# A mixture-of-experts trunk on one core: PSUM handed over in two halves, and slot tables from one-hot products on chip

## The chip, the cores and the metric

The kernel runs on one core of a Trainium2 chip. The metric is the time of one execution in microseconds (us), as the device reports it. The engines are TensorE (PE, with its weight loads as PEld), VectorE (DVE), ScalarE (ACT), GpSimd (POOL) and SyncE (SP, which here only issues DMAs). Each runs its own instructions strictly in the order in which they were written, and waits on semaphores for the others.

## The reference

The layer takes x of 512 tokens by 1024 columns, mixes tokens by three head groups (a state space, pooling, block-sparse attention), adds the result to x, and then adds a mixture of experts. The second part, to which the change belongs, is this:

```python
t = rms_norm(x, norm2_g).reshape(-1, dm)
g_logits = t @ group_w + group_b              # 4 groups
g_sel = argmax(g_logits); g_wt = softmax(g_logits)[g_sel]
e_logits = (t @ router_w + router_b)[g_sel]   # 4 experts of that group
top_v, top_i = top_k(e_logits, 2); top_w = softmax(top_v)
comb[g_sel, top_i] = g_wt * top_w             # 512 x 16, two nonzero per token
act = silu(t @ w_gate[e]) * (t @ w_up[e]) * comb[:, e]
x = x + sum_e act @ w_down[e]
out = rms_norm(x, final_norm_g)
```

There are 16 experts with 256 hidden columns each. Their weights are 48 MB in float32 and are read once.

## The kernel before

**Slots and units.** Each expert has room for 96 token copies, so there are 1536 slots, handled as 12 units of 128. The 512 tokens are 4 tiles of 128, m = 0 to 3. Routing (`s_route`, line 1259) finds for each tile and each of a token's two choices i the slot number: `sv`, as float, and `slot_i`, as integer. A token's activations are kept as two float16 halves (`hl`, high and low), and every float32 product is made in three float16 passes.

**How tokens get to the slots.** Units 0 and 1 are gathered on chip: TensorE multiplies `hl` by one-hot matrices `sel`. Unit 0 (`s_gather`, line 1404) sums in four PSUM banks `gb` and is copied to `xts`; unit 1 (`s_gather_all`, line 1415) sums in four banks `gc` and is copied by ACT and DVE to `xp` (the rows show this buffer's earlier name). For units 2 to 11 GpSimd scatters the rows of `hl` into `x_scr` in DRAM (`scatter`, line 1250), and SP loads them back as `xr`; TensorE transposes them (`tx`).

**How a slot's token and weight are found.** The triple (row of the result, combining weight, token) of each token and choice is `mt_`. `s_meta_out` (line 1458) scatters the triples with eight indirect DMAs of GpSimd, 12 bytes a row, to `m_scr` in DRAM, which `s_clear` (line 804) has filled from an input with the values of an empty slot. `s_meta` (line 1643) loads the table back as `mt` and makes `tok` (the row to which a slot's result is scattered), `cw` (its weight), and `hot_e`, one-hot matrices for the last two units, from it.

**The expert stage.** For each unit u, `s_gate_up` (line 1584) multiplies the unit by gate and up weights into a PSUM bank `pg`; ACT and DVE make silu and product (`xs`); TensorE transposes it (`pta`); ACT and DVE split it into float16 halves (`aT`); TensorE multiplies by the down weights (`py`, two halves); ACT or DVE scales by `cw` into `ys`, and GpSimd scatters `ys` to `y_scr` in DRAM (`y_out`).

**The weights.** They come as 96 loads of 512 KB, six per expert, into five staging buffers `st_lde`. `st_lde_2_1` is the second half of the third matrix. ACT makes the high float16 half, DVE (a few times GpSimd) the low half, with one instruction each; only then is the staging buffer free for the load five places on. In this text gu5_0_1 is the split of expert 5's gate weights, second half.

**PSUM.** Up to the experts one pool `psA` holds all eight banks (`mm` x 3, `at` x 2, `tr` x 2, `po`; function `bank`). When routing is done and unit 1 is gathered, `s_memory` (line 1815) closes it and opens `psB` with `pg`, `pta`, `py`, `tx`.

**What sets the order.** A planner, class `Flow` (line 97), writes each engine's instructions. Every stage is a generator that yields an engine, the events that it needs and the tokens (buffers) that it takes; the planner always takes the one that its cost model would start first, with the rank that the stage was spawned with to break near ties. So an edit in one place can move instructions elsewhere. The real waits are semaphores, set from what each instruction reads and writes; and nearly all instructions of the trace carry the planner's line, L89.

Of the kernel before, what the change touches and what calls it, by code (L numbers as in the profile page):

```python
# [9 lines left out]
F16 = mybir.dt.float16  # L10
# [9 lines left out]
P = 128  # L20
D = 1024
# [40 lines left out]
C_W = C_COL + P  # L62
# [211 lines left out]
def hybrid_trunk_kernel(tc, a, out, cap=CAPACITY, dbg=None):  # L274
# [38 lines left out]
    m_scr = dram.tile([NSLOT + 2 * S, 3], F32, name="m_scr")  # L313
# [7 lines left out]
    phE, phP, phR, phQ, phA, phX = (ES() for _ in range(6))  # L321
# [29 lines left out]
    psA = phA.enter_context(tc.tile_pool(name="psA", bufs=1, space=PSUM))  # L351
    BANKS = {"mm": 3, "at": 2, "tr": 2, "po": 1}
    for k_, n_ in BANKS.items():
        fl.tokens(k_, n_)

    def bank(tag, name):
        return psA.tile([P, 512], F32, tag=tag, name=name, bufs=BANKS[tag])

# [435 lines left out]
    def s_clear():  # L794
# [9 lines left out]
        sp.dma_start(m_scr[0:NSLOT, :], a["meta0"])  # L804
# [442 lines left out]
    pads = cst.tile([P, 4 * NT + NE], F32, name="pads")  # L1247
# [11 lines left out]
    def s_route(m):  # L1259
        xg, h2T = (R_[m][k] for k in ("xg", "h2T"))  # L1260
        if m == 0:
            M["sm"] = M["R"].tile([P, NT, 170], F32, name="sm_r")
            M["sel"] = M["R"].tile([P, NT, NG, P], F16, name="sel")
# [12 lines left out]
        pool.tensor_scalar(rs16, rs, SA, None, ALU.mult)  # L1276
        fl.spawn(3, hl_out(m, xg, rs16))
# [5 lines left out]
        if m == NT - 1:  # L1283
# [7 lines left out]
        gm, kg, mg = R("gm", 1), R("kg", 4), R("mg", 4)  # L1291
# [8 lines left out]
        v.tensor_scalar(mg, kg, gk, -1.0, ALU.is_equal, ALU.add)  # L1300
        yield "dve"
        v.scalar_tensor_tensor(ms16.rearrange("p (g e) -> p g e", g=4),
                               mg.unsqueeze(2).to_broadcast([P, 4, 4]), -NEG,
# [28 lines left out]
        ok, sl, jk, sv = R("ok", 16), R("sl", 16), R("jk", 32), R("sv", 2)  # L1332
# [35 lines left out]
        yield "pool", (("hl", m),)  # L1368
# [26 lines left out]
    def gathered(g, banks, toks):  # L1395

        xT = xT_[g] = xts[0] if g == 0 else x2_t[NT - 1].bitcast(F16).rearrange("p (c n) -> p c n", n=P)
        for i, b in enumerate(banks):
            yield "dve" if i % 2 else "act"
# [15 lines left out]
    def s_gather_all(g):  # L1415

        toks = ("at", "at", "tr", "tr")
        yield "pe", (("gather", g - 1, NT - 1), "flag", ("acc", NT - 1)), toks
# [11 lines left out]
    def s_gates():  # L1430

        lg, gm, m8, ok, sl = (F_[n] for n in ("lg", "gm", "m8", "ok", "sl"))
        ge, gs, dn, co = (M["sm"][:, :, a_:b_] for a_, b_ in ((150, 155), (155, 156), (156, 157), (57, 89)))
# [15 lines left out]
        fl.spawn(0, s_meta_out())  # L1449
# [126 lines left out]
    def xt_out(u, h, tx, left):  # L1576
        yield "dve" if h else "act"
        (v.tensor_copy if h else act.copy)(xT_[u][:, h * KD:(h + 1) * KD, :], tx)
        fl.give("tx")
# [4 lines left out]
    def s_gate_up():  # L1584
        for u in range(NU):
            es = [e for e, _, _ in owners(u)]
            yield "pe", (("xT", u),) + tuple(("we", e, i) for e in es for i in range(2)), ("pg",)
            pg = B["ps"].tile([P, 512], F32, tag="pg", name=f"pg{u}", bufs=2)
# [14 lines left out]
    def s_down(u, pg):  # L1603
        ex_p, ps = B["ex"], B["ps"]
        es = [e for e, _, _ in owners(u)]
        ends = [e for e in es if last_unit[e] == u]
        yield "act", (), ("ex",)
# [8 lines left out]
        pt = ps.tile([P, 2 * P], F32, tag="pta", name=f"pta{u}")  # L1616
# [3 lines left out]
        yield "act"  # L1620
        aT = ex_p.tile([P, 2, 2, P], F16, tag="aT", name=f"aT{u}")
# [5 lines left out]
        ys = ex_p.tile([P, D], F32, tag="ys", name=f"ys{u}")  # L1627
        for nh in range(2):
            if nh and u < NU - 2:
                yield "pe"  # L1630
            py = ps.tile([P, 512], F32, tag="py", name=f"py{u}_{nh}", bufs=3)
# [8 lines left out]
        fl.give("ex")  # L1640
        fl.sig(*(("dend", e) for e in ends))

    def s_meta():
        yield "pool", ("meta", "B")
        mt = B["ex"].tile([P, NU, 3], F32, tag="mt", name="mt", bufs=1)
        pool.dma_start(mt, m_scr[0:NSLOT, :].rearrange("(u c) w -> c u w", c=P))
        fl.sig_dma("mt")
        yield "dve", ("mt",)
        B["tok"] = B["ex"].tile([P, NU], I32, tag="tok", name="tok", bufs=1)
        B["cw"] = B["ex"].tile([P, NU], F32, tag="cw", name="cw", bufs=1)  # L1650
        v.tensor_copy(B["tok"], mt[:, :, 0])
        v.tensor_scalar(B["cw"], mt[:, :, 1], ISC, None, ALU.mult)
        fl.sig("cw")
        for i in range(NL):
            for t in range(NT):
                yield "dve", (("dend", NE - 5),)
                if i == 0 and t == 0:
                    B["hot"] = page("p3", [P, NL, S], F16, "hot_e")
                v.tensor_scalar(B["hot"][:, i, t * P:(t + 1) * P], cpk[:, C_COL:C_COL + P],
                                mt[:, NU - NL + i, 2:3], -float(t * P), ALU.subtract, ALU.is_equal)  # L1660
# [103 lines left out]
    def y_out(u, nh, py, ys):  # L1764
# [19 lines left out]
        else:  # L1784
# [12 lines left out]
            fl.sig_dma(("y1", u))  # L1797


    phB, ph0 = ES(), ES()  # L1800

    def s_memory():
        yield "mem", ("dm", "epn", "sprev")
# [212 lines left out]
```

## Time and profile before

| | us |
|---|---|
| median of 3 runs | 458.46 |
| lowest, highest | 454.86, 460.24 |
| the profiled execution's own time | 455.13 |
| span of that execution | 453.3 |

| engine | busy us | share of the span |
|---|---|---|
| PE | 374.5 | 83% |
| DVE | 318.3 | 70% |
| PEld | 208.2 | 46% |
| ACT | 248.4 | 55% |
| POOL | 116.7 | 26% |

The mean granted clock of TensorE is 0.931 of full speed. 109.88 MB move by DMA, 242 GB/s over the span. The shares are means over parts of the kernel that have different limits; the part that the change touches lies between 255 and 320 us, so windows and timelines of that part say more than the totals. Start times in the rows count from the span's start. A pause stands in square brackets behind the row that ended it, with what released it; "remote" means that no other engine's or DMA's end was found for it.

### The profile page before, as it was taken

What the parts mean: (1) busy time and instruction counts of PE and PEld (TensorE: products, weight loads), DVE (VectorE), ACT (ScalarE), POOL (GpSimd) and SP (SyncE); (2) the same over time, 40 slices, a digit from 0 to 9 for tenths busy, and PEclk for the clock granted to TensorE, in tenths of its full rate; (3) what the DMA queues carried; (4) which work ended last, traced back from release to release, by engine and by line L of the source; (5) the groups of instructions that cost most, each with busy time, mean ns of one, the idle gap of its engine ahead of it and who ended that gap; (6) DMA issues with size and microseconds to landing.
All of it is one profiled execution on the core that took longest, in us unless ns stands there. A gap on an engine that the chain in (4) does not pass through costs nothing. (4 is left out here: it accounts for less than half of the span.)

```text
span 453.3 us, 8911 instructions
## 1 busy us (share of the span) xinstructions
PE 374.5 (83%) x3456; PEld 208.2 (46%) x3456; DVE 318.3 (70%) x638; ACT 248.4 (55%) x399; POOL 116.7 (26%) x202
## 2 busy tenths in 40 slices
PE   2899964399999999989999673699999795858992
PEld 1697531164446456444466463254545342413340
DVE  2789807955785877976689991548678778877383
ACT  4753203143658986875776530348677677575231
POOL 1248984402400100011117458003111001000010
PEclk9999995889999999999999668699999999969997
DMA  8912549998698598674395442558999999988933
GB/s 283 339 50 38 76 55 261 383 337 272 191 167 271 187 317 281 213 232 137 114 353 190 161 181 94 170 207 249 413 410 328 418 354 350 314 309 313 406 134 142
DMA packets 49153, 109.88 MB, mean 242 GB/s; under 512 B 4499, under 2 KB 25907, under 8 KB 49108
## 3 DMA queue, kind: packets, MB, share of 16 engines
q1 hardware_dynamic: 45652, 99.57, 66.8%
q0 software_dynamic: 2896, 9.47, 5.5%
q8 instruction: 28, 0.46, 0.4%
q10 hardware_dynamic: 560, 0.25, 0.3%
q14 instruction: 17, 0.14, 0.1%
HBM read 83.59 MB, written 25.70 MB: 241 GB/s over the span
## 5 line engine op out<-in xcount | busy, mean ns | idle before, releaser
L89 DVE SCALAR_TENSOR_TENSOR gu<-st_lde,gu 128x1024 f16<-128x1024 f32 x63 | 76.9, 1236 | 19.3 <-ACT gu L89 19.2
L89 PE MATMUL pg<-gu,xts 128*32 128x512 f16 (+1 forms) x912 | 64.9, 392 | 13.1 <-DVE xp L89 11.5
L89 ACT ACTIVATE gu<-st_lde 128x1024 f16<-128x1024 f32 x64 | 66.4, 1054 | 16.3 <-DMA st_lde<-in_moe_w_gate_dram 8.7
L89 PEld LDWEIGHTS <-xts 128*32 128x32 f16 (+1 forms) x912 | 28.0, 101 | 44.8 <-issue 22.0
L89 PE MATMUL px<-wo,cat 128*128 128x512 f16 x192 | 44.7, 379 | 0.0
L89 PE MATMUL py<-dn,aT 128*32 128x512 f16 (+1 forms) x480 | 37.9, 406 | 5.5 <-ACT aT L89 4.8
L89 DVE SCALAR_TENSOR_TENSOR dn<-st_lde,dn 128x1024 f16<-128x1024 f32 x30 | 37.5, 1256 | 5.9 <-ACT dn L89 5.9
L89 ACT ACTIVATE dn<-st_lde 128x1024 f16<-128x1024 f32 x32 | 33.2, 1054 | 7.2 <-DMA st_lde<-in_moe_w_down_dram 7.0
L89 PEld LDWEIGHTS <-hT 128*64 128x64 f16 (+1 forms) x384 | 31.2, 156 | 6.7 <-issue 2.9
L89 POOL DMA_INDIRECT y_scr<-ys,tok x10 | 10.4, 1040 | 87.7 <-ACT ys L89 84.4
L89 PE MATMUL ps_k<-hT,w_k 128*128 128x512 f16 x96 | 24.3, 406 | 10.0 <-ACT qk L89 10.0
L89 ACT ACTIVATE pr<-pr,nm 128x128 f32<-128x128 f32 (+3 forms) x32 | 17.9, 558 | 25.3 <-DVE nm L89 25.0
L89 PEld LDWEIGHTS <-cat 128*128 128x128 f16 x192 | 18.2, 99 | 21.3 <-issue 3.2
L89 PEld LDWEIGHTS <-aT 128*32 128x32 f16 (+1 forms) x480 | 14.1, 103 | 26.3 <-ACT aT L89 6.6
L89 PE MATMUL ps_v<-w_v,hT 128*128 128x256 f16 x192 | 24.7, 287 | 0.8 <-ACT hT L89 0.4
L89 PE MATMUL psS<-qk 64*64 64x128 f32 (+3 forms) x128 | 24.0, 474 | 0.0
L89 PE MATMUL ptp<-cpk,pr 128*128 128x128 f32 x80 | 14.9, 289 | 9.8 <-DVE rcp L89 7.0
L89 ACT COPY pts<-ptp 128x128 f32<-128x128 f32 (+3 forms) x32 | 13.4, 422 | 17.6 <-PE ptp L89 17.3
L89 PE MATMUL ps_q<-hT,w_q 128*128 128x512 f16 x96 | 22.6, 379 | 0.0
L89 POOL TENSOR_TENSOR dn<-st_lde,dn 128x1024 f16<-128x1024 f32 x2 | 4.9, 2463 | 65.8 <-ACT dn L89 65.8
L89 PEld LDWEIGHTS <-w_k 128*128 128x128 f16 x96 | 9.4, 102 | 22.4 <-issue 13.8
L89 PEld LDWEIGHTS ptp<-cpk,pr 128*128 128x128 f32 x80 | 9.2, 142 | 19.3 <-issue 15.5
(255 smaller groups left out, 715.1 us busy)
## 6 DMA issues: line engine op xcount, KB each, us to landing
st_lde<-in_moe_w_gate_dram SPq DMA_DIRECT2D x32, 512.0 KB
st_lde<-in_moe_w_up_dram SPq DMA_DIRECT2D x32, 512.0 KB
st_lde<-in_moe_w_down_dram SPq DMA_DIRECT2D x32, 512.0 KB
x_scr<-zero SPq DMA_DIRECT2D x12, 512.0 KB
xr<-x_scr SPq DMA_DIRECT2D x10, 512.0 KB
xp<-in_x_dram SPq DMA_DIRECT2D x8, 512.0 KB
y_scr<-zero SPq DMA_DIRECT2D x8, 512.0 KB
yr<-y_scr SPq DMA_DIRECT2D x4, 1024.0 KB
```

Of the source, the lines that this page charges most:

```text
L89: r = f(*args, **kw)
```

## The change

1. The PSUM pool is split. `psA` (banks `mm`, `po`) and `psC` (`at`, `tr`) take its place; at the hand-over `psB` (`pg` x 2, `pta`, `tx0`) opens once unit 0's copies are planned, and `psD` (`py` x 3, `tx1`) once routing, the new slot table and unit 1's copies are.
2. `m_scr`, its load, the eight scatters and the load back are gone. `s_places` makes on DVE, from the slot numbers `sv_`, one-hot rows: `place` (which of a unit's 128 slots) and `vals` (which unit, times the triple); eight float32 matmuls sum place x vals into a PSUM tile `pm`, 128 slots by 36 columns. `s_meta` reads `cw`, `tok` and the tokens for `hot_e` from `pm` by four DVE instructions. The constants `cpk` grow by 25 columns.
3. The scatters of tiles 1 and 2 on GpSimd wait until the last tile's 1/rms has been computed there.
4. The wait for the store of x2 to DRAM moves from unit 1's gather to its copies.

```diff
-    psA = phA.enter_context(tc.tile_pool(name="psA", bufs=1, space=PSUM))
+
     BANKS = {"mm": 3, "at": 2, "tr": 2, "po": 1}
+    HALF = {"mm": 0, "po": 0, "at": 1, "tr": 1, "pg": 0, "tx0": 0, "py": 1, "pta": 0, "tx1": 1}
+    psum = [es.enter_context(tc.tile_pool(name=n_, bufs=1, space=PSUM, side=s_))
+            for es, n_, s_ in ((phA, "psA", "left"), (phA2, "psC", "right"))]
...
-        sp.dma_start(m_scr[0:NSLOT, :], a["meta0"])
...
+        fl.sig(("rms", m))
...
-        yield "pool", (("hl", m),)
+        yield "pool", (("hl", m),) + ((("rms", NT - 1),) if m in (1, 2) else ())
...
-    def s_meta_out():
-        for m in range(NT):
-            yield "pool"
-            for i in range(2):
-                scatter(m, m_scr, mt_[:, m, i, :], i)
-        fl.sig_dma("meta")
+    def s_places():
+
+        K = 2 * NT
+        yield "dve", ("B0",), ("R", "R")
...
+        v.tensor_tensor(ge, sv.to_broadcast([P, K, NU + 1]), edge.unsqueeze(1).to_broadcast([P, K, NU + 1]), ALU.is_ge)
+        yield "dve"
+        v.tensor_reduce(cnt_u, ge, AX.X, ALU.add)
+        v.scalar_tensor_tensor(col, cnt_u, -float(P), sv, ALU.mult, ALU.add)
+        yield "dve"
+        v.tensor_tensor(oneh, ge[:, :, 0:NU], ge[:, :, 1:NU + 1], ALU.subtract)
+        yield "dve"
+        v.tensor_tensor(vals.rearrange("p k (w u) -> p k w u", w=3), oneh.unsqueeze(2).to_broadcast([P, K, 3, NU]),
+                        mt_.rearrange("p t i w -> p (t i) w").unsqueeze(3).to_broadcast([P, K, 3, NU]), ALU.mult)
+        for k in range(K):
+            yield "dve"
+            v.tensor_scalar(A[:, k], cpk[:, C_COL:C_COL + P], col[:, k], float(P), ALU.subtract, ALU.is_equal)
+        yield "pe", (), ("tx0",)
+        B["pm"] = psum[HALF["tx0"]].tile([P, 512], F32, tag="tx0", name="pm")
+        for k in range(K):
+            pe.matmul(B["pm"][:, 0:3 * NU], A[:, k], vals[:, k], start=(k == 0), stop=(k == K - 1))
+        fl.sig("placed")
...
     def s_meta():
-        yield "pool", ("meta", "B")
-        mt = B["ex"].tile([P, NU, 3], F32, tag="mt", name="mt", bufs=1)
-        pool.dma_start(mt, m_scr[0:NSLOT, :].rearrange("(u c) w -> c u w", c=P))
-        fl.sig_dma("mt")
-        yield "dve", ("mt",)
...
-        v.tensor_copy(B["tok"], mt[:, :, 0])
-        v.tensor_scalar(B["cw"], mt[:, :, 1], ISC, None, ALU.mult)
+        etok = B["ex"].tile([P, NL], F32, tag="etok", name="etok", bufs=1)
+        junk = B["ex"].tile([P, NU], F32, tag="junk", name="junk", bufs=1)
+        rows, gate, toks = (B["pm"][:, i * NU:(i + 1) * NU] for i in range(3))
+        v.tensor_scalar(B["cw"], gate, ISC, None, ALU.mult)
+
+        v.scalar_tensor_tensor(junk, rows, 0.0, cpk[:, C_JUNK:C_JUNK + NU], ALU.is_equal, ALU.mult)
+        v.scalar_tensor_tensor(B["tok"], rows, -1.0, junk, ALU.add, ALU.add)
+        v.tensor_copy(etok, toks[:, NU - NL:])
+        fl.give("tx0")
...
-        yield "mem", ("routed", ("xT", NG - 1))
+        yield "mem", (("xT", 0),)
+        fl.t = fl.ev["gather", 0, NT - 1]
+        phA.close()
+        psum[0] = phB0.enter_context(tc.tile_pool(name="psB", bufs=1, space=PSUM, side="left", reuse_waits="tile"))
+        for k_, n in (("pg", 2), ("pta", 1), ("tx0", 1), ("aT0", 1)):
+            fl.tokens(k_, n)
+        fl.sig("B0")
+        yield "mem", ("routed", "placed", ("xT", NG - 1))
         fl.t = fl.ev["gather", NG - 1, NT - 1]
```

The order of instructions moves in three places that matter here. On DVE, from the end of routing (`cov`) to the first product of unit 0 (`xs`), the kernel before has this; `gc` are unit 1's gather banks, `st_lde` the weight halves of expert 5:

```order
L89 TENSOR_TENSOR cov<-sm_r 128x4x16
L89 CAST tri_89<-cpk 128x128
L89 CAST xp_120<-gc_1_2977 128x512
L89 SCALAR_TENSOR_TENSOR gu_1_2759<-st_lde_0_1_2545,gu_0_2758 128x4x256
L89 CAST xp_120<-gc_3_2979 128x512
L89 SCALAR_TENSOR_TENSOR gu_1_2759<-st_lde_1_0_2560,gu_0_2758 128x4x256
L89 SCALAR_TENSOR_TENSOR gu_1_2759<-st_lde_1_1_2570,gu_0_2758 128x4x256
L89 SCALAR_TENSOR_TENSOR dn_3063<-st_lde_2_0_2641,dn_3063 128x1024
L89 SCALAR_TENSOR_TENSOR xs_121<-pg_3090,xs_121 128x256
```

And the changed kernel, from the small `vals` instructions to the next weight split:

```order
L91 CAST xp_122<-gc_1_2974 128x512
L91 TENSOR_TENSOR vals<-vals 128x96
L91 TENSOR_TENSOR vals<-vals,mt__137 128x288
L91 CAST xp_122<-gc_3_2976 128x512
L91 TENSOR_SCALAR place<-cpk,vals 128x128 x8
L91 SCALAR_TENSOR_TENSOR gu_1_2756<-st_lde_0_0_2539,gu_0_2755 128x4x256
L91 SCALAR_TENSOR_TENSOR xs_123<-pg_3061,xs_123 128x256
L91 TENSOR_SCALAR cw<-pm 128x12
L91 SCALAR_TENSOR_TENSOR junk<-pm,cpk 128x12
L91 SCALAR_TENSOR_TENSOR tok<-pm,junk 128x12
L91 COPY etok<-pm 128x2
L91 SCALAR_TENSOR_TENSOR gu_1_2756<-st_lde_0_1_2556,gu_0_2755 128x4x256
```

The weight splits stand one half later than before, the eight `place` and the four readings of `pm` stand among them, and `xs` of unit 0 stands ahead of four weight splits that it followed.

On PE, behind the last matmul of unit 0's `pg`, the changed kernel has the eight matmuls of `pm`, and then unit 1's `pg`:

```order
L91 MATMUL pg_3061<-gu_1_1791,xts_124 32x512
L91 MATMUL pm<-vals,place 128x36 x8
L91 LDWEIGHTS xp_122
L91 MATMUL pg_3190<-gu_0_1790,xp_122 64x512
L91 LDWEIGHTS xp_122
```

Before, unit 1's `pg` followed unit 0's directly. On POOL, the changed kernel has the last tile's 1/rms (four instructions, the first of which reads `ss`) ahead of the scatters of `x_scr` from tiles 1 and 2 (`slot_i`):

```order
L91 TENSOR_TENSOR xg_2732<-xp_122,g_1783 128x512
L91 TENSOR_TENSOR sm_r<-ss_85 128x1
L91 TENSOR_SCALAR sm_r<-sm_r 128x1
L91 TENSOR_TENSOR sm_r<-sm_r,nhalf 128x1
L91 TENSOR_SCALAR sm_r<-sm_r 128x1
L91 MEMSET pads 128x1
L91 DMA x_scr<-xp_121,slot_i 2560x2048
L91 MEMSET pads 128x1
L91 DMA x_scr<-xp_121,slot_i 2560x2048
```

Before, the first two of these scatters stood between `xg` and the four instructions.

## Rows read from the trace of the kernel before

**Rows 1.** The page's busy tenths of the whole span in 40 slices of 11.3 us each.

```profile
PE   2899964399999999989999673699999795858992
DVE  2789807955785877976689991548678778877383
DMA  8912549998698598674395442558999999988933
```

**Rows 2.** The view of windows: start:end, length, busy us of each engine (with the number of instructions), granted clock of TensorE, mean share of the DMA engines, GB/s.

```profile
270.00:280.00 10.00, 5.93 (x69) 5.85 (x70) 3.56 (x20) 0.69 (x2) 7.70 (x15) 0.79 0.30 109
280.00:290.00 10.00, 2.33 (x24) 1.03 (x27) 4.80 (x6) 4.24 (x5) 4.02 (x6) 0.56 0.19 20
...
320.00:390.00 70.00, 59.49 (x831) 28.71 (x824) 55.78 (x71) 49.98 (x62) 7.75 (x13) 0.98 1.00 378
```

**Rows 3.** The view of waits for 268 to 292 us: who waited for whom, total us, times, longest.

```profile
ACT xp L89 <- remote: 13.1, 1, 13.1
PE pg L89 <- DVE xp L89: 11.5, 1, 11.5
DVE xp L89 <- remote: 11.4, 1, 11.4
```

**Rows 4.** The timeline of PE: start, length, engine, line, operation, output <- inputs, count, and in brackets the pause before it and its releaser.

```profile
275.14 1.06 PE L89 MATMUL gc<-sel,hl 128*128 128x128 f16 x16
287.67 7.16 PE L89 MATMUL pg<-gu,xts 128*32 128x512 f16 x96 [11.48 <-DVE xp L89]
```

**Rows 5.** The timeline of ACT.

```profile
284.47 0.58 ACT L89 CAST xp<-gc 128x512 f16<-128x512 f32 x1 [13.12 <-remote]
```

**Rows 6.** The timeline of DVE, from routing's end to the first product of unit 0.

```profile
273.55 0.22 DVE L89 CAST tri<-cpk 128x128 f16<-128x128 f32 x1
285.19 0.69 DVE L89 CAST xp<-gc 128x512 f16<-128x512 f32 x1 [11.43 <-remote]
285.80 1.22 DVE L89 SCALAR_TENSOR_TENSOR gu<-st_lde,gu 128x1024 f16<-128x1024 f32 x1
...
289.80 1.22 DVE L89 SCALAR_TENSOR_TENSOR dn<-st_lde,dn 128x1024 f16<-128x1024 f32 x1
295.30 0.42 DVE L89 SCALAR_TENSOR_TENSOR xs<-pg,xs 128x256 f32<-128x256 f32 x1 [4.28 <-ACT xs L89]
```

**Rows 7.** The timeline of POOL: the first and the last of the eight `m_scr` scatters, and a weight split.

```profile
273.50 0.97 POOL L89 DMA_INDIRECT m_scr<-mt__134,slot_i  x1 [0.19 <-DVE sm_r L89]
...
282.35 0.96 POOL L89 DMA_INDIRECT m_scr<-mt__134,slot_i  x1 [0.19 <-issue]
...
309.86 2.80 POOL L89 TENSOR_TENSOR dn<-st_lde,dn 128x1024 f16<-128x1024 f32 x1 [22.63 <-ACT dn L89]
```

**Rows 8.** The DMA view of 276 to 284 us: all packets that moved in it.

```profile
DMA packets 223, 0.01 MB, mean 1 GB/s; under 512 B 223, under 2 KB 223, under 8 KB 223
```

**Rows 9.** The timeline of SP: the weight load 6_0_0, and the loads of the scattered rows of units 2 and 3.

```profile
287.08 0.35 SPq L89 DMA_DIRECT2D st_lde<-in_moe_w_gate_dram  x1
287.60 0.80 SPq L89 DMA_DIRECT2D xr<-x_scr  x2
```

**Rows 10.** Durations that serve as prices: PE's `pg` of unit 2 (two pieces) and `pl` of the first and the last tile, from its timeline; a DVE reading of 12 columns, from its timeline; and, from the view by tile, eight DVE one-hot instructions (ns: least, median, most; first and last start).

```profile
307.37 3.64 PE L89 MATMUL pg<-gu,xts 128*32 128x512 f16 x64
312.35 1.91 PE L89 MATMUL pg<-gu,xts 128*32 128x512 f16 x32
230.64 1.86 PE L89 MATMUL pl<-rw,h2T 128*128 128x20 f32 x16
257.17 3.58 PE L89 MATMUL pl<-rw,h2T 128*128 128x20 f32 x16
308.58 0.17 DVE L89 TENSOR_SCALAR cw<-mt 128x12 f32<-128x12 f32 x1
L89 DVE TENSOR_SCALAR hot_e<-cpk,mt x8: 274/283/325, 388.4 to 389.8; 128x128 f16<-128x128 f32 x8
```

**Rows 11.** The timeline of DVE, from unit 0's `aT` to the first split of expert 7, the rows with pauses and one copy.

```profile
299.42 0.42 DVE L89 SCALAR_TENSOR_TENSOR aT<-pta,aT 128x256 f16<-128x256 f32 x1 [1.43 <-ACT aT L89]
301.15 0.42 DVE L89 SCALAR_TENSOR_TENSOR xs<-pg,xs 128x256 f32<-128x256 f32 x1 [1.31 <-ACT xs L89]
304.69 1.23 DVE L89 SCALAR_TENSOR_TENSOR gu<-st_lde,gu 128x1024 f16<-128x1024 f32 x1 [3.12 <-ACT gu L89]
...
306.17 0.68 DVE L89 COPY xts<-tx 128x1024 f16<-128x1024 f16 x1
...
312.47 0.75 DVE L89 TENSOR_SCALAR ys<-py,cw 128x512 f32<-128x512 f32 x1 [1.80 <-PE py L89]
...
314.26 1.22 DVE L89 SCALAR_TENSOR_TENSOR gu<-st_lde,gu 128x1024 f16<-128x1024 f32 x1
```

**Rows 12.** The timeline of DVE: the last split of expert 15's down weights.

```profile
417.44 1.22 DVE L89 SCALAR_TENSOR_TENSOR dn<-st_lde,dn 128x1024 f16<-128x1024 f32 x1
```

**Rows 13.** The timelines of POOL and DVE around the last tile's 1/rms: a scatter, the first rms instruction, and DVE's logits of that tile.

```profile
257.25 2.65 POOL L89 DMA_INDIRECT x_scr<-xp,slot_i  x1
259.92 0.20 POOL L89 TENSOR_TENSOR sm_r<-ss 128x1 f32<-128x1 f32 x1
...
261.48 0.23 DVE L89 SCALAR_TENSOR_TENSOR sm_r<-pl,sm_r,rbias 128x20 f32<-128x20 f32 x1
```

More of the change, by code (lines that the diff above doesn't have):

```diff
@@ L61 @@
 C_COL = C_ELIM + NE
-C_W = C_COL + P
+C_EDGE = C_COL + P
+C_JUNK = C_EDGE + 13
+C_W = C_JUNK + 12
 def _free(ap):
@@ L319, in hybrid_trunk_kernel @@
     t_scr = dram.tile([8, HD * (VW + 1)], F32, name="t_scr")
-    phE, phP, phR, phQ, phA, phX = (ES() for _ in range(6))
+    phE, phP, phR, phQ, phA, phA2, phX = (ES() for _ in range(7))
     cst = pool_of(top, "cst")
@@ L356, in bank @@
     def bank(tag, name):
-        return psA.tile([P, 512], F32, tag=tag, name=name, bufs=BANKS[tag])
+        return psum[HALF[tag]].tile([P, 512], F32, tag=tag, name=name, bufs=BANKS[tag])
     gp_ = pool_of(phQ, "gp_", 1, "right")
@@ L1246, in hybrid_trunk_kernel @@
     F_ = {}
-    pads = cst.tile([P, 4 * NT + NE], F32, name="pads")
+    pads = cst.tile([P, 2 * NT + NU], F32, name="pads")
+    sv_ = cst.tile([P, NT, 2], F32, name="sv_")
     mt_ = cst.tile([P, NT, 2, 3], F32, name="mt_")
@@ L1456, in s_gates, with part @@
         fl.sig("routed")
-    def s_meta_out():
-        for m in range(NT):
-            yield "pool"
-            for i in range(2):
-                scatter(m, m_scr, mt_[:, m, i, :], i)
-        fl.sig_dma("meta")
+    def s_places():
+        K = 2 * NT
+        yield "dve", ("B0",), ("R", "R")
+        A, W = (M["R"].tile([P, D], F32, tag="xg", name=n, bufs=2) for n in ("place", "vals"))
+        A = A.rearrange("p (k c) -> p k c", k=K)
+        def part(c0, n):
+            return W[:, c0:c0 + K * n].rearrange("p (k n) -> p k n", k=K)
+        ge, cnt_u, col = part(0, NU + 1), part(K * (NU + 1), 1), part(K * (NU + 2), 1)
+        oneh, vals = part(K * (NU + 3), NU), part(K * (2 * NU + 3), 3 * NU)
+        sv = sv_.rearrange("p t i -> p (t i)").unsqueeze(2)
+        edge = cpk[:, C_EDGE:C_EDGE + NU + 1]
+        v.tensor_tensor(ge, sv.to_broadcast([P, K, NU + 1]), edge.unsqueeze(1).to_broadcast([P, K, NU + 1]), ALU.is_ge)
[15 more added lines that the diff above has]
+        fl.sig("placed")
     def hl_out(m, xg, rs16):
@@ L1615, in s_down @@
         yield "pe", (), ("pta",)
[L1616 removed]
+        pt = psum[HALF["pta"]].tile([P, 2 * P], F32, tag="pta", name=f"pta{u}")
         acv = ac.rearrange("p (c k) -> p k c", k=2)
@@ L1626, in s_down @@
         fl.sig(*(("dstart", e) for e in ends))
-        ys = ex_p.tile([P, D], F32, tag="ys", name=f"ys{u}")
+        ys = B["ex"].tile([P, D], F32, tag="ys", name=f"ys{u}")
         for nh in range(2):
@@ L1630, in s_down @@
                 yield "pe"
-            py = ps.tile([P, 512], F32, tag="py", name=f"py{u}_{nh}", bufs=3)
+            py = psum[HALF["py"]].tile([P, 512], F32, tag="py", name=f"py{u}_{nh}", bufs=3)
             i = 0
@@ L1817, in s_memory @@
         phQ.close()
-        phA.close()
+        phA2.close()
         B["ex"] = pool_of(phB, "ex", 2, "right")
         xts.extend(B["ex"].tile([P, 2 * KD, P], F16, name=f"xts{i}", bufs=1) for i in range(1, NXT))
-        B["ps"] = phB.enter_context(tc.tile_pool(name="psB", bufs=1, space=PSUM, reuse_waits="tile"))
-        for k_, n in (("pg", 2), ("pta", 1), ("py", 3), ("tx", 2), ("ex", 2), ("ys", 2)):
+        psum[1] = phB.enter_context(tc.tile_pool(name="psD", bufs=1, space=PSUM, side="right", reuse_waits="tile"))
+        for k_, n in (("py", 3), ("tx1", 1), ("aT1", 1), ("ys", 2)):
             fl.tokens(k_, n)
```

57 lines of the change are left out of this document (29 added, 28 removed).

## The prediction, made before the changed kernel was run

> **What bounds the kernel now.** I read the page's busy tenths first [rows 1], then ten-microsecond windows around the change [rows 2], then the list of waits of that stretch [rows 3], then the timelines of the engines there. The tenths show three regimes: TensorE nearly full until about 250 us, a dip after it, and from about 290 us a stretch in which the 16 DMA engines are full. The windows say how deep the dip is: in 270:280 and 280:290 the DMA share is 0.30 and 0.19, TensorE works 5.93 and 2.33 us of ten, and no engine is full in 280:290. In 320:390 the DMA share is 1.00: there the kernel takes the expert weights as fast as they come, so time lost in the dip is not won back later, nor is time won in the dip lost.
>
> In the waits one pause shows on three engines at once: PE 11.5, DVE 11.4, ACT 13.1 us [rows 3]. TensorE's row of gather matmuls for unit 1 (`gc`) ends at 276.20, and its next row, `pg` of unit 0, begins at 287.67 [rows 4]. What stands between them are the four copies of `gc` into `xp`. But ACT's first copy begins at 284.47 and DVE's at 285.19 [rows 5, 6], both "remote", 8 to 9 us after the matmuls' shown end, with nothing running on either engine. The one thing that fills these 8 us is GpSimd: eight `m_scr` scatters of about 0.96 us each from 273.50 on, the last at 282.35 [rows 7]; and the DMA view of 276:284 holds 223 packets with 0.01 MB, all from that queue [rows 8]. The sync engine's next weight load is issued only at 287.08 [rows 9], since the buffer it needs is freed by the DVE split at 285.80 [rows 6].
>
> **The change part by part, forecast.** I take it that the copies' start is tied to the `m_scr` scatters, and that it goes with them. For it: the scatters' packets fill just this pause, and an `x_scr` scatter such as that at 257.25, with far larger rows, runs beside a `pl` of TensorE whose result DVE reads 0.73 us after its end (260.75 to 261.48) [rows 10, 13].
>
> *PSUM halves.* `pg0` no longer needs the banks of `gc`, so it follows `gc` on TensorE at 276.2. Its price: `pg` of the unit behind took 3.64 + 1.91 = 5.55 us at full granted clock [rows 10], `pg0` itself 7.16 at a clock that was at the lower level (0.56 granted in 280:290, after the pause) [rows 2, 4]. With no pause ahead of it I take 5.55, 7.16 as the other end: `pg0` ends at 281.75 instead of 294.83, 13.1 earlier.
>
> *Places on VectorE.* After the shown end of `tri` at 273.77 [rows 6] it gets three small instructions (at most 0.3 each, as the 128x128 ones of rows 10) beside `gc`. From 276.2 on: copy 0.69, `oneh` 0.3, the 128x288 product (between 0.28 and the copy's 0.69; I take 0.69, the nearer in width), copy 0.69, eight `place` at 0.283 = 2.26 [rows 6, 10]: done at 280.8, under `pg0`. The split `gu5_0_0` ends at 282.0, `xs` from `pg0` at 282.6.
>
> *`pm`.* Eight fp32 matmuls with 36 columns. The nearest row is `pl`, eight fp32 matmuls (16 records) with 20 columns: 1.86 at the upper clock level, 3.58 at the lower [rows 10]. I take 1.86: 281.75 to 283.6. The four readings of `pm` stand on VectorE **ahead of the weight splits**; four times 0.17 (the `cw` row [rows 10]) gives 284.3, and the split behind them, `gu5_0_1`, ends at 285.5. It frees the buffer of the load of 6_0_0; before, that split ended at 287.02 [rows 6].
>
> *VectorE to the first split of expert 7.* From 285.5, in the new order: two `aT` and two `xs` at 0.42 (1.68), two `xts` at 0.68 (1.36), two `ys` at 0.75 (1.50), and eleven splits at 1.22 (13.42), of which one, `dn6_2_0`, ran on GpSimd before (2.80 us at 309.86 [rows 7]); 17.96 in all [rows 6, 11]. Back to back that ends at 303.5. Before, the stretch from 291.02 (end of the split at 289.80) to 314.26 held 11.94 us of pauses: 4.28 for `pg0`'s `xs`, which goes, and 1.43 + 1.31 + 3.12 + 1.80 = 7.66 for later matmuls and loads [rows 6, 11]. How much of the 7.66 stays no row shows: 0 to 7.66; I keep 4.5, rather over half, since `pg1`, `py` and the loads keep their lengths and only start sooner. The split of 7_0_0 then ends at 308.0 instead of 315.48 (314.26 + 1.22): **7.5 us earlier**, between 4.3 (all of 7.66 stays) and 12.0 (none stays).
>
> *Carrying it to the end.* From that split to the last, at 417.44 [rows 12], lie 53 others in 103.2 us, 1.95 each, in a stretch with DMA share 1.00: the whole of it shifts. TensorE follows the weights and closes the kernel behind them, at 9 tenths in the slices from 419 to 442 [rows 1]. I carry all 7.5.
>
> *The rest, at nothing.* The last tile's rms goes ahead of the scatters of tiles 1 and 2 on GpSimd. Its four rows begin at 259.92, right behind a scatter of 2.65 us, but DVE's `lg` at 261.48 also needs `pl`, on TensorE until 260.75 [rows 10, 13]: at most 0.7 is to be had. The scatters behind it slip by the 1.7 us of rms and whatever rms waits for; what they feed is loaded at 287.60 [rows 9], over 20 us later, and that cover hides them. Two more weight splits that GpSimd did go to VectorE long before the dip (2 x 1.22); VectorE is not full there in most tenths [rows 1], so 0, with +2.4 as the bound. The planner also reshuffles TensorE's attention part; with the same work, I bound it at 2 us either way, taken as 0. The first `y_scr` scatters come forward out of the full DMA stretch, which can only help a little: 0 to -1.
>
> **Sum.** 455.13 - 7.5 = 447.6 against the profiled execution. The median of the three runs, 458.46, stands 3.3 above that; measured from it the forecast is **451.0**.
>
> **The rivals.** *(b) The whole pause is won.* Nothing of the 7.66 stays and the PE wait of 11.5 is all gain: 458.46 - 11.5 = 447. For it: VectorE's pauses there are mostly waits for TensorE. Against: the eleven splits and the eight `place` do not shrink.
>
> *(c) The message stays late, TensorE is free.* The cause is not the scatters of `m_scr`; the copies still begin at 284.5 and 285.2, while `pg0` runs in the pause. Then DVE does copy, `oneh`, product, copy, `place` from 285.2 to 289.8, `pm` ends at 291.7, the readings at 292.4, `gu5_0_1` at 293.6; with the same 17.96 + 4.5 the split of 7_0_0 ends at 316.0, 0.6 later than before: **459**. What TensorE won is given back by VectorE. For it: "remote" names no cause, and a coincidence in time is all that ties the pause to the scatters.
>
> *(d) Slower: TensorE itself is late.* If `gc` really runs until 285, `pg0` is behind it at the lower clock level: 285.2 + 7.16 = 292.4, and `pm` comes after that, at the lower level 3.58: 296.0; the four readings and `gu5_0_1` end at 297.9, where before a split had freed that buffer at 287.02 without waiting for any matmul. With 17.96 + 4.5 the split of 7_0_0 ends at 320.4, 4.9 later: **463.4** (461.7 with `pm` at 1.86). It decides from the point where `pg0` ends later than about 288, since 7.5 is then used up. For it: the readings put a wait for TensorE ahead of the weight stream, which stood free of it. Against: the granted clock in 280:290 is 0.56, and TensorE's next work, `pg0`, was still at the lower level, as after a real pause [rows 2, 4]; matmuls that ran until 285 would rather have held it up.
>
> The row says 276.20 for the end of `gc` and 284.47 for the first copy. The Trainium skill, in "Perfetto Trace Analysis", section "Tensor Engine Instruction (MATMUL, LD_WEIGHTS)", says that a matmul's end in a profile is worked out from its size, and that the semaphore goes out only once PSUM has acknowledged the writes, which the profile doesn't show. By that rule the 276.20 need not be the end, and the sum would be rival (d)'s; by the row alone it would be the forecast's.
>
> **How the numbers follow.** Forecast 0.45, (b) 0.13, (c) 0.22, (d) 0.20. About 1% (4.6 us: under 453.9, over 463.0) is what a measurement of this kernel can tell. Faster by over 1%: nine tenths of the forecast and all of (b), 0.54, say 0.55. Slower by over 1%: about half of (d) and a reshuffle that goes wrong on top of (c), 0.15. Within 1%: 0.30. The range: the forecast's bounds are 458.46 - 12.0 = 446.5 and 458.46 - 4.3 = 454.2; with a microsecond for the attention part below, and up to (c) with a microsecond above it, 445.5 to 460. Left out are (d) and the outer ends, about 2 in 10. The likeliest case's own range is 446.5 to 454.
>
> **What would show it.** Right: the `gc` copies begin within 1.5 us of the matmuls' shown end; `pg` has no wait of 11 us; `pg0` is near 5.6 us; the DMA share in 280:290 is well over 0.19; `pm` is near 1.9 and the readings of it wait little. The copies' start decides: near 277 is the forecast or (b), near 285 is (c) if `pg0` ran in the pause, (d) if `pg0` is behind it. The term most likely mis-sized is the 4.5 us of pauses that I keep. The prediction is wrong altogether if the pause just moves to the readings of `pm`, or if the attention part ends some microseconds elsewhere: then `gc` itself does not start near 270.8.

## The result, and the profile after

| | runs | median us | lowest, highest |
|---|---|---|---|
| before | 13 | 459.17 | 454.86, 463.17 |
| changed | 13 | 453.81 | 450.52, 458.96 |

The ratio is 0.9883, 95% interval 0.9844 to 0.9922: 5.4 us faster (3.6 to 7.2). The forecast was 451.0, with a range of 445.5 to 460.0. The profiled execution of the changed kernel took 457.71 us, one of its slowest, and that of the kernel before (455.13) one of its fastest; so stages are compared here from a common mark, the start of `gc`, at 270.77 before and 277.28 after, and not span against span.

What decided the forecast is the message from `gc` to its copies. The timelines of PE, ACT and DVE of the changed kernel, in that order:

```profile
277.28 4.11 PE L91 MATMUL gc<-sel,xp 128*128 128x128 f16 x48
281.22 1.06 PE L91 MATMUL gc<-sel,hl 128*128 128x128 f16 x16
282.21 5.36 PE L91 MATMUL pg<-gu,xts 128*32 128x512 f16 x96
287.50 1.97 PE L91 MATMUL pm<-vals,place 128*128 128x36 f32 x16
```

```profile
281.64 0.58 ACT L91 CAST xp<-gc 128x512 f16<-128x512 f32 x1 [3.79 <-PE gc L91]
```

```profile
281.87 0.69 DVE L91 CAST xp<-gc 128x512 f16<-128x512 f32 x1 [1.05 <-PE gc L91]
...
283.74 1.65 DVE L91 TENSOR_SCALAR place<-cpk,vals 128x128 f32<-128x128 f32 x8
...
288.04 0.42 DVE L91 SCALAR_TENSOR_TENSOR xs<-pg,xs 128x256 f32<-128x256 f32 x1 [1.52 <-ACT xs L91]
289.51 0.17 DVE L91 TENSOR_SCALAR cw<-pm 128x12 f32<-128x12 f32 x1 [1.05 <-PE pm L91]
...
289.95 1.22 DVE L91 SCALAR_TENSOR_TENSOR gu<-st_lde,gu 128x1024 f16<-128x1024 f32 x1
...
313.10 1.22 DVE L91 SCALAR_TENSOR_TENSOR gu<-st_lde,gu 128x1024 f16<-128x1024 f32 x1
```

Before, the first copy began 8.27 us after the shown end of `gc` and was marked remote [rows 4, 5]. Now it begins at 281.64, when the first of the four banks is done and 0.64 us before the last matmul's end, and its releaser is named: PE. `pg0` follows `gc` with no pause, in 5.36 us; the granted clock in 280:290 is at the upper level (before, 0.56 in [rows 2]), and TensorE is busy all ten microseconds of it:

```profile
280.00:290.00 10.00, 10.00 (x159) 6.79 (x158) 6.28 (x24) 3.68 (x5) 0.00 (x0) 1.00 0.34 120
```

The split of 7_0_0 ends at 314.32, 37.04 after the start of `gc`; before, it ended at 314.26 + 1.22 = 315.48 [rows 11], so 315.48 - 270.77 = 44.71. That is 7.7 us, where 7.5 was forecast.

One sign that the prediction named for being wrong did come: `gc` itself starts at 277.28, not near 270.8. Counting from `gc` leaves these 6.5 us out; the last section comes back to them.

### The profile page after: what moved, and what is told of

It is laid out like the page before. It is cut to its first block, busy times and chain, and to the rows that moved or that the text cites. A ratio compares the mean times of both kernels' runs of the same rounds, so it can differ in the third digit from the quotient of the medians.

```text
span 455.8 us, 8926 instructions
## 1 busy us (share of the span) xinstructions
PE 379.3 (83%) x3472; PEld 210.9 (46%) x3472; DVE 322.4 (71%) x656; ACT 245.0 (54%) x396; POOL 102.2 (22%) x182
## 5 line engine op out<-in xcount | busy, mean ns | idle before, releaser
L91 PE MATMUL py<-dn,aT 128*32 128x512 f16 (+1 forms) x480 | 40.3, 418 | 4.3 <-ACT aT L91 3.4
L91 POOL DMA_INDIRECT y_scr<-ys,tok x10 | 12.5, 1246 | 115.8 <-ACT ys L91 87.0
L91 PE MATMUL ps_k<-hT,w_k 128*128 128x512 f16 x96 | 23.3, 395 | 11.0 <-ACT qk L91 11.0
L91 POOL TENSOR_TENSOR xg<-xp,g 128x512 f32<-128x512 f32 x4 | 6.1, 1515 | 100.9 <-DVE nm L91 96.4
L91 PEld LDWEIGHTS <-aT 128*32 128x32 f16 (+1 forms) x480 | 14.7, 106 | 26.8 <-issue 7.7
```

Of the source, the lines that this page charges most:

```text
L91: r = f(*args, **kw)
```

## The experiments

Each run is the changed kernel with one edit, except where it says otherwise. "Lead" is how much earlier a mark comes than in the profile before, both counted from the start of `gc`.

### A second profile, and the rms part undone

The first has no edit. The second:

```diff
-        yield "pool", (("hl", m),) + ((("rms", NT - 1),) if m in (1, 2) else ())
+        yield "pool", (("hl", m),)
```

> The changed kernel unaltered, for a second profile beside the other runs. Theory A (the gain is the vanished late message, less some loss ahead of it): gc copies again begin within 1.5 us of the shown end of gc, no 11 us wait at pg; time near 453.8, ratio to the kernel before 0.985 to 0.992. Whether the 6.5 us by which the first profile's routing started late (pl of the first tile at 237.5 against 230.6) is the changed order of the attention part or that one execution: if the order, pl of the first tile again starts at 237 or later; if the execution, within 2 us of 231.

> The changed kernel without its third part: the scatters of tiles 1 and 2 no longer wait for the last tile's 1/rms. Prediction's view: at most 0.7 us, so the time is that of the changed kernel within 1 us. Rival (the moved rms is worth more, since VectorE's xp product and GpSimd's scatters hinder each other): the last tile's logits come 2 us or more later and the time rises by 2 us or more.

Unaltered: 456.31 us (4 runs), ratio 0.9896 (0.9779 to 1.0012); `gc` ends at 281.67 and ACT's copy begins at 281.04, so the message is in time again. `pl` of the first tile began at 236.0, by the expectation's test near the "order" side; but later runs with the very same order on PE, DVE, ACT and SP began it at 229.5 to 231.8. So it is not the order of these engines. But all five of those runs have the table `m_scr` in DRAM again, which this one has not, so whether it is the execution or the table is open; it is taken up at the end.

Without the rms part: 452.49 us (4 runs), ratio 0.9882 (0.9811 to 0.9953), the changed kernel's own. The rms part is worth nothing that can be measured, as forecast (at most 0.7 us); the rival of 2 us is out.

### Scatters put back: eight small, eight wider, eight plain, four small

Behind the last scatter of `x_scr`, on GpSimd alone and hidden from the planner, so that all other engines keep their order. The rows written are never read.

```diff
+        if m == NT - 1:
+            more = []
+            for t in range(NT):
+                for i in range(2):
+                    nc.gpsimd.memset(pads[:, ...], 0.0)
+                    ins = nc.gpsimd.indirect_dma_start(
+                        out=m_scr[:, :], out_offset=bass.IndirectOffsetOnAxis(ap=slot_i[:, t, i:i + 1], axis=0),
+                        in_=cpk[:, 0:3], in_offset=None)
```

The wider ones have `cpk[:, 0:128]`; four of them, `range(2)`; the plain ones, `nc.gpsimd.dma_start(m_scr[r_:r_ + P, :], cpk[:, 0:3])`.

> The changed kernel with eight added scatters of 12-byte rows on GpSimd (constants, to a DRAM table nobody reads) behind the last scatter of x_scr, everything else in the same order. Theory A (such scatters hold back TensorE's message that gc is done): the gc copies begin 5 to 9 us after the shown end of gc, marked remote, while pg of unit 0 follows gc at once; place, pm and the split behind them come that much later; time 3 to 8 us above the changed kernel. Rival (the late message came from the single PSUM hand-over or the wait at pg, not from the scatters): the copies begin within 1.5 us of the end of gc and the time is that of the changed kernel within 1.5 us.

> As the run with eight 12-byte scatters, but with rows of 512 bytes. If it is the count of scatters that GpSimd issues: copies 5 to 9 us late here too. If it is the small packets: the copies begin within 1.5 us of the end of gc and the time is that of the changed kernel within 1.5 us.

> As the run with eight 12-byte scatters, but with eight plain DMAs of GpSimd of the same size instead of indirect ones. If it is GpSimd's DMAs as such: TensorE again executes pg of unit 0 in pieces and the gc copies begin 5 us or more late, 6 to 10 us above the changed kernel. If it takes the indirect ones: gc copies within 1.5 us, time as the changed kernel within 2 us.

> As the run with eight 12-byte scatters, but four. Theory A': TensorE stands still from some 2 us behind the first of them until the last has landed; with four of them, 1.27 us apart, the gc copies begin about 5 us earlier than with eight, 1 to 4 us late, and the time is 2 to 5 us above the changed kernel. Rival (a fixed price once the queue has taken more than a few): as with eight, 8 us above.

| added on GpSimd | median us | ratio to before | first copy after `gc`'s end, us | `pg0` start to end, us |
|---|---|---|---|---|
| nothing (changed kernel) | 453.81 | 0.9883 | -0.64 | 5.36 |
| eight indirect, 12 bytes | 462.39 | 1.0091 (1.0056 to 1.0127) | 8.29 | 15.69 |
| eight indirect, 512 bytes | 462.78 | 1.0091 (1.0057 to 1.0126) | 6.92 | 13.85 |
| eight plain, 12 bytes | 451.39 | 0.9847 (0.98 to 0.9894) | -0.63 | 5.36 |
| four indirect, 12 bytes | 454.89 | 0.9908 (0.9871 to 0.9944) | 3.07 | 7.98 |

With the eight 12-byte scatters, PE's timeline shows what neither the trace of before nor the prediction did:

```profile
272.30 0.89 PE L91 MATMUL gc<-sel,hl 128*128 128x128 f16 x13
274.17 0.33 PE L91 MATMUL gc<-sel,hl 128*128 128x128 f16 x3 [0.98 <-issue]
274.43 0.39 PE L91 MATMUL pg<-gu,xts 128*32 128x512 f16 x1
275.62 0.42 PE L91 MATMUL pg<-gu,xts 128*32 128x512 f16 x3 [0.81 <-issue]
277.04 0.42 PE L91 MATMUL pg<-gu,xts 128*32 128x512 f16 x3 [1.00 <-issue]
277.77 0.43 PE L91 MATMUL pg<-gu,xts 128*32 128x512 f16 x1 [0.30 <-issue]
278.48 3.42 PE L91 MATMUL pg<-gu,xts 128*32 128x512 f16 x6 [0.28 <-issue]
282.72 7.40 PE L91 MATMUL pg<-gu,xts 128*32 128x512 f16 x82 [0.82 <-issue]
```

Beside them on POOL, the last tile's two scatters of `x_scr` and the first and the last of the eight added ones, and ACT's copy:

```profile
268.43 0.98 POOL L91 DMA_INDIRECT x_scr<-hl,slot_i  x1 [4.37 <-DVE mt__138 L91]
269.71 0.95 POOL L91 DMA_INDIRECT x_scr<-hl,slot_i  x1 [0.19 <-issue]
270.98 0.97 POOL L1382 DMA_INDIRECT m_scr<-cpk,slot_i  x1 [0.19 <-issue]
...
279.85 0.96 POOL L1382 DMA_INDIRECT m_scr<-cpk,slot_i  x1 [0.19 <-issue]
```

```profile
282.79 0.59 ACT L91 CAST xp<-gc 128x512 f16<-128x512 f32 x1 [13.97 <-remote]
```

From 273.2, some 2.2 us behind the start of the first added scatter, to 282.7, 1.9 us behind the last one's end, TensorE issues 17 matmuls: 3 of `gc` and 14 of `pg0` in handfuls, with pauses marked "issue", in which nothing that the profile shows holds it; from 282.72 on the other 82 run through. The first copy, which needs only `gc`, begins at 282.79. So two things are held at once: TensorE's own instructions and the messages that it sends. Theory A holds and is too narrow, since it had TensorE free. The two scatters of `x_scr` run at the same pace just ahead of the eight, so the row is of ten, as in the kernel before (from 270.96 on there), and of six with four added. The two by themselves, which the changed kernel has too (277.47 and 278.75), do nothing of the kind: in none of the seven profiles without added or `m_scr` scatters is a pause of TensorE marked "issue".

The width does not matter: 512-byte rows cost the same, so it is not the small packets. That GpSimd issues DMAs does not matter either: eight plain ones, 0.54 to 0.61 us each and through within 5.3 us, leave TensorE alone, and the time is 2.4 us under the changed kernel's, just beyond the 2 expected and with an overlapping interval. It takes the indirect ones in a row. With four, TensorE was held for about 3 us and the time is only some 1 us above the changed kernel, below the 2 to 5 expected, with an overlapping interval. The nearer mark for all of these is the run with plain ones: it too has the table `m_scr` in DRAM, and its order on PE, DVE and ACT is the same. Above its 451.39, eight indirect ones cost 11.0 us and four 3.5, though the intervals of the last two overlap.

### The halves alone, and the table alone

The halves alone are the kernel before, slot table through DRAM and all, with the split pools of the change (the diff's parts on `psum`, `HALF`, `tx0`, `tx1`, `aT0`, `aT1` and `s_memory`; the table's and the rms part are left out, and the moved wait for the store of x2, part 4, stays in). The table alone is the changed kernel with

```diff
-    HALF = {"mm": 0, "po": 0, "at": 1, "tr": 1, "pg": 0, "tx0": 0, "py": 1, "pta": 0, "tx1": 1}
+    HALF = {"mm": 0, "po": 0, "at": 1, "tr": 1, "pg": 1, "tx0": 0, "py": 0, "pta": 1, "tx1": 1}
...
-        for k_, n in (("pg", 2), ("pta", 1), ("tx0", 1), ("aT0", 1)):
+        for k_, n in (("py", 3), ("tx0", 1), ("aT0", 1)):
...
-        for k_, n in (("py", 3), ("tx1", 1), ("aT1", 1), ("ys", 2)):
+        for k_, n in (("pg", 2), ("pta", 1), ("tx1", 1), ("aT1", 1), ("ys", 2)):
```

so that `pg0` takes banks of `gc` and waits for the copies, the table and `pm`; once so, and once with the rms part undone as well.

> The kernel before with the PSUM halves alone: the slot table still goes through the eight scatters and the load back, rms in the old place, the orders nearly those of the kernel before. Theory A (the scatters stop TensorE itself, so a free bank is of no use): pg of unit 0 starts near the end of gc but runs in pieces with pauses marked issue until the last scatter has landed, gc copies 5 to 9 us late, marked remote; time that of the kernel before (458 to 460) within 3 us. Rival (what waits is only the copies): pg of unit 0 is done within 8 us of the end of gc, and the time falls by 3 us or more, to 455 or less.

> The changed kernel with pg, pta and tx1 in the half of PSUM that unit 1's gather leaves, and py in the other: so pg of unit 0 must again wait for the gc copies, the slot table and pm, as with one hand-over; no scatters of the slot table. Theory A (the late message was the loss, the halves only hide the copies): pg of unit 0 starts 5 to 8 us after the end of gc instead of at once; the split of 7_0_0 comes 3 to 6 us later counted from the start of gc; time 3 to 5 us above the changed kernel, so level with the kernel before or just under it. Rival (the split hand-over carries the gain): 6 us or more above the changed kernel, slower than the kernel before.

> The table from one-hot products alone: as the run with pg in the right half (pg of unit 0 waits for the gc copies again), and with the rms part undone as well. Theory A (leaving out the row of scatters is the whole gain, the halves add nothing): 450 to 454, level with or under the changed kernel (453.8), 1% or more under the kernel before; gc copies within 1.5 us of the end of gc. Rival (the split is worth something after all): 2 us or more above the changed kernel, 456 or more.

The halves alone: 458.27 us (10 runs), ratio 0.9975 (0.9935 to 1.0015), no change. Its PE timeline, and ACT's copy:

```profile
278.19 0.39 PE L89 MATMUL pg<-gu,xts 128*32 128x512 f16 x1
278.77 0.38 PE L89 MATMUL pg<-gu,xts 128*32 128x512 f16 x1 [0.19 <-issue]
...
283.03 1.32 PE L89 MATMUL pg<-gu,xts 128*32 128x512 f16 x3 [0.81 <-issue]
285.16 7.12 PE L89 MATMUL pg<-gu,xts 128*32 128x512 f16 x85 [0.81 <-issue]
```

```profile
285.25 0.59 ACT L89 CAST xp<-gc 128x512 f16<-128x512 f32 x1 [13.96 <-remote]
```

`pg0` has its bank and its inputs from 278.2 on, and still 85 of its 96 matmuls run only from 285.16, when the scatters are through. The bank alone was not what it lacked.

The table alone: 452.83 us (4 runs, two near 449 and two near 457, too spread for an interval), and without the rms part 453.08 us (6 runs), ratio 0.9892 (0.9847 to 0.9938): the changed kernel's time. The first missed what was expected of it, 3 to 5 us above the changed kernel with `pg0` 5 to 8 us behind the end of `gc` and 7_0_0 3 to 6 us later: `pg0` began 3.8 us behind, and 7_0_0 ended 32.4 after the start of `gc`, 4.6 us earlier than in the changed kernel. In the second `pg0` starts late, as it should:

```profile
277.02 1.06 PE L91 MATMUL gc<-sel,hl 128*128 128x128 f16 x16
279.96 3.24 PE L91 MATMUL pm<-vals,place 128*128 128x36 f32 x16 [1.88 <-DVE place L91]
283.14 7.34 PE L91 MATMUL pg<-gu,xts 128*32 128x512 f16 x96
```

It starts 5.1 us after the end of `gc` and takes 7.3 us (the granted clock fell to the lower level in it; in the first run it stayed at the upper, and `pg0` took 5.36), so that it ends 18.5 us after the start of `gc` (290.48 - 271.97) where the changed kernel's ends 10.3 after it (287.57 - 277.28), and yet the split of 7_0_0 ends 35.8 after the start of `gc`, earlier than the changed kernel's 37.0. So the changed kernel's early `pg0` buys nothing further: the gain is the copies' message and TensorE set free, and that comes from the table. (The planner moves other instructions between the two, splits among them, so the 1.2 us is no measure of the halves.)

### The same scatters in the expert stage

The eight 12-byte scatters, put behind unit 4's result (`if u == 4:` in `y_out`) instead of behind routing.

> The changed kernel with the eight added 12-byte scatters placed behind unit 4's result in the expert stage instead of behind routing. Theory A (a row of indirect scatters holds TensorE up wherever it stands): PE shows a run of pauses marked issue of some 6 to 9 us in all, beside the scatters, and the messages of its matmuls come late; time 4 to 9 us above the changed kernel, less what the weight stream would have made it wait anyway. Rival (it is a matter of that place: the end of routing, few packets, an idle queue): TensorE goes on as it does without them, time as the changed kernel within 2 us.

453.46 us (10 runs), ratio 0.99 (0.9865 to 0.9934): the changed kernel's time, so the expected 4 to 9 us above it are not there. The hold is not gone altogether. PE and ACT beside the last of the scatters (332.35 to 344.54):

```profile
342.79 0.80 PE L91 MATMUL pg<-gu,xts 128*32 128x512 f16 x7
343.78 0.42 PE L91 MATMUL pg<-gu,xts 128*32 128x512 f16 x4 [0.18 <-issue]
344.52 3.54 PE L91 MATMUL pg<-gu,xts 128*32 128x512 f16 x53 [0.32 <-issue]
```

```profile
345.46 0.69 ACT L91 ACTIVATE ys<-py,cw 128x512 f32<-128x512 f32 x1 [4.27 <-remote]
```

One message was late, for a `py` that PE shows ended at 342.97, and two short pauses are marked issue. But most matmuls went through beside the scatters. That they cost nothing isn't shown, though: the stretch from the split of 7_0_0 to that of 10_1_1, in which they lie, takes 46.5 us here and 42.8 to 44.3 in the nine other profiles with the same order there, and the time is 2.1 us above that of the run with plain scatters (453.46, 451.39; the intervals overlap). So the price is smaller here and hangs on what runs beside the scatters; whether it is the full DMA queues, which spread these scatters over 12.2 us instead of 9.8, or what stood waiting, this run doesn't tell.

### Where the lead goes in the expert stage

In all profiles of kernels in the changed kernel's order the lead fell by several microseconds between the splits of 12_1_1 and 12_2_0 (expert 12's second up half, "12u1", and first down half, "12d0"). There VectorE's timeline, here of the run without the rms part, has `hot_e` and its wait ahead of the down splits:

```profile
377.91 0.75 DVE L91 TENSOR_SCALAR ys<-py,cw 128x512 f32<-128x512 f32 x1 [1.27 <-PE py L91]
379.58 1.66 DVE L91 TENSOR_SCALAR hot_e<-cpk,etok 128x128 f16<-128x128 f32 x8 [0.92 <-PE py L91]
381.17 2.35 DVE L91 SCALAR_TENSOR_TENSOR dn<-st_lde,dn 128x1024 f16<-128x1024 f32 x2
```

Two runs move `hot_e`, the first in the changed kernel, the second with the rms part undone as well:

```diff
-                yield "dve", (("dend", NE - 5),)
+                yield "dve", (("dend", NE - 3),)
```

> The changed kernel with the eight hot_e instructions put behind expert 12's end instead of expert 10's, so that they no longer stand on VectorE ahead of the two splits of 12's down weights. Counted from the start of gc, the changed kernel's lead over the kernel before falls there from 6 to 8 us (at 12u1) to 2 to 3 us (at 12d0) in all profiles. Theory B (hot_e and its wait for TensorE hold the splits and so the loads): the lead at 12d0 stays at 5 us or more, the end comes 2 to 3 us earlier than the changed kernel's, time 450 to 452. Rival (the DMA queue sets it whatever stands there): the lead falls all the same, time as the changed kernel within 1 us.

The second has `NE - 4`.

> The changed kernel without the rms part, and with hot_e behind expert 11's end (one later than it was), where it stands ahead of expert 14's up splits and no longer waits for a matmul that is still running. Theory B (the stream's give-back is hot_e's place: at 10's end it held 12's down splits by some 2.5 us, at 12's end it held the last down split by some 3 us): from 7_0_0 to the last split 103 to 105 us, as in the kernel before (103.2), instead of 105.8 to 106.9; end some 2 us earlier than the run without rms, time 450 to 452. Rival (the weight stream gives back the lead whatever VectorE's order is): 105.5 us or more again, time 452 to 454.

| ends of splits, us from the start of `gc` | 7_0_0 | 12u1 | 12d0 | last | `7_0_0` to last |
|---|---|---|---|---|---|
| before | 44.7 | 110.6 | 112.7 | 147.9 | 103.2 |
| changed | 37.0 | 104.0 | 109.4 | 143.5 | 106.5 |
| changed, second profile | 38.4 | 105.3 | 111.1 | 145.3 | 106.9 |
| no rms part | 37.6 | 104.4 | 110.1 | 143.3 | 105.8 |
| `hot_e` behind 12 | 37.9 | 104.6 | 107.7 | 144.7 | 106.8 |
| `hot_e` behind 11, no rms part | 38.2 | 105.6 | 108.7 | 145.5 | 107.3 |
| eight plain scatters | 38.0 | 105.4 | 111.1 | 144.5 | 106.5 |
| eight indirect, 12 bytes | 48.6 | 116.5 | 122.4 | 155.6 | 106.9 |
| halves alone | 42.3 | 110.0 | 115.4 | 149.2 | 106.9 |

(Each number is the end of that split in DVE's timeline less the start of `gc`.) The local reading was right: with `hot_e` away, the step from 12u1 to 12d0 takes 3.1 us in both instead of 5.4 to 5.8 in the changed kernel's order, and the lead at 12d0 was 5.0 and 4.0. It didn't help: with `hot_e` behind 12 it stands ahead of the very last split,

```profile
412.70 0.67 DVE L91 TENSOR_SCALAR hot_e<-cpk,etok 128x128 f16<-128x128 f32 x3
413.96 0.75 DVE L91 SCALAR_TENSOR_TENSOR ys<-py,cw,ys 128x512 f16<-128x512 f32 x1 [0.59 <-ACT ys L91]
414.63 1.06 DVE L91 TENSOR_SCALAR hot_e<-cpk,etok 128x128 f16<-128x128 f32 x5
415.61 1.22 DVE L91 SCALAR_TENSOR_TENSOR dn<-st_lde,dn 128x1024 f16<-128x1024 f32 x1
```

which then ends 4.7 us after the one before it; and with `hot_e` behind 11 the whole stretch still takes 107.3 us. The times are 453.16 us (12 runs, 0.9896, 0.9864 to 0.9928) and 452.10 us (6 runs, 0.9863, 0.9823 to 0.9903), neither apart from the changed kernel's 0.9883. Theory B falls as far as the time goes. What makes this stretch 2.6 to 4.1 us longer than the one profile of the kernel before stays open: the bytes in it don't (36.54 MB before, 35.97 in the second profile of the changed kernel), its rate does (354 and 336 GB/s), and that one profile is of an execution 4 us under its kernel's median, so some of the difference may be that execution. Two things in the table speak for that. The 103.2 us stand alone among all fourteen profiles: the others take 105.8 to 109.7, the halves alone 106.9 too, which has the old scatters and the kernel before's time. And between two runs with the same order on PE, DVE and ACT nothing is given back: the eight indirect scatters put 7_0_0 10.6 us later than the plain ones do, the last split 11.1 later, and the time is 11.0 longer.

## Why the prediction was right, and where it was not

**The cause of the pause: right, and shown.** The forecast rested on the copies' start being tied to the `m_scr` scatters. Taken out, the message is in time in every profile; put back alone, it is 8.3 us late again and costs 8.6 us (453.81 to 462.39), or 11.0 against the run with plain scatters in their place.

**PSUM halves: the wrong part was given the gain.** The prediction's first term was `pg0` 13.1 us earlier because it "no longer needs the banks of `gc`". The sizes were near (`pg0` 5.36 us, forecast 5.55; `pm` 1.97, forecast 1.86). But the halves alone give 0.9975, and the table without them gives the full gain. In the step "it follows `gc` on TensorE at 276.2", the wait for banks hid a second one: with the bank free, TensorE itself was held.

**VectorE up to the first split of expert 7: right in sum, by errors that cancelled.** `place` took 1.65 us for 2.26, the 128x288 product 0.46 for 0.69; `gu5_0_1` ended 13.9 us after the start of `gc` (14.7 forecast), after a wait of 1.05 for `pm`. The pauses behind it came to 6.1 us, not the 4.5 kept, but with the work shorter 7_0_0 came at 37.0, forecast 37.2 (308.0 - 270.77).

**Carrying it to the end: 2.1 us too many, from a place that stays open.** "I carry all 7.5." The lead at 7_0_0 was 7.7, 6.4 and 7.1 us in the three profiles of the table above without a moved `hot_e`, and at the last split 4.4, 2.6 and 4.6; the measured gain is 5.4. Against this one profile of the kernel before, then, 2.6 to 3.8 us were given back. The DMA share of 1.00 in 320:390 [rows 2] was taken to make the stretch rigid, which is too strong: over the whole stretch the mean share is 0.96 before and 0.93 to 0.95 after, and moving `hot_e` alone shortened the step from 12u1 to 12d0 by over 2 us. But that a lead doesn't carry isn't shown, since the profile of before is the odd one and the pair of runs with indirect and plain scatters kept its 10.6 us to the end. The other place for the missing 2.1 us is ahead of `gc`, where the sum had nothing (next point).

**The rest at nothing: right for the rms part, open for the others.** Without the rms part the time is the same (452.49). The splits moved to VectorE, the reshuffled attention part and the earlier `y_scr` scatters were not tried by themselves. `gc` started 1.5 to 6.5 us later than before in the three profiles of the changed kernel with and without the rms part, where the prediction had bounded the attention part at 2; as far as that belongs to the change, it is a loss that the sum left out.

**The rivals.** (b), the whole pause, 447: out, since 6.1 us of pauses stayed where it had none. (c), the message late but TensorE free, and (d), TensorE late too: neither came, as the scatters were the cause; but the runs with scatters put back show what they would have been, a mixture: the message late as in (c), and TensorE held as in (d), by pauses and not by long matmuls. The Trainium skill's rule in "Perfetto Trace Analysis", section "Tensor Engine Instruction (MATMUL, LD_WEIGHTS)", that a matmul's shown end is worked out, was weighed as ground for (d). In the run with eight 12-byte scatters `pg`'s first matmul starts at 274.43, so `gc` had by then been issued whole, 8.4 us ahead of the copy. The late message fits what the page says of the unseen acknowledgement, though no run tells a late acknowledgement from a late message; an end of `gc` near 285, as (d) had it, the trace doesn't bear out.

## What to carry to other kernels

When two engines sit "remote" behind a matmul that looks finished, see what else runs in just those microseconds, and put the suspect back into the fast kernel with every other engine's order kept: that told cause from bystander here in one run, where four edits had come in one change. An edit that removes a wait should also be run alone; this one's first part removed a wait that was not the one that counted. And one profile is one execution: a stretch that seemed to give back a lead was measured against a single profile of the kernel before, while two runs that differ only ahead of that stretch kept their difference through it.

## What the hardware showed that was not expected

A row of ten indirect DMAs of GpSimd, 1.27 us apart (two of `x_scr`, then eight), held TensorE almost still for some 9 us (17 matmuls, in a time in which all 96 of `pg0` would have run) and kept back its messages until the last had landed; with rows of 512 bytes as with 12. Eight plain DMAs of the same engine and size did not, pairs of `x_scr` scatters by themselves show no such pause, and beside a full weight stream the price was smaller, 2.1 us above the run with plain ones and not clear of the noise. What it is in the chip that is shared stays open.

The start of `gc` moved from 268.2 to 277.3 between profiles of kernels whose order ahead of it is the same or nearly so. The seven profiles of kernels that have the table `m_scr` in DRAM, read or not, lie at 268.2 to 271.8, the seven without it at 271.3 to 277.3. That may be chance, or the place of the other tables in DRAM; no run tried it by itself. If it is the tables, the change itself costs some microseconds ahead of `gc`, and the gain that the forecast missed lies there: the run with plain scatters, which has the table again, took 451.39, near the 451.0 that was forecast.
